# FFN down projection by seven products of block sums in place of eight, alternated with the next block's up products; pieces of 328, 356, 356 tokens

## The chip, the cores and the metric

The kernel runs on one core of one Trainium2 chip. The metric is device time in microseconds (us) of one execution. Before the change three runs took 2256.22, 2258.66 and 2259.83 us; the median is 2258.66. One further execution was recorded by the hardware profiler, and all rows of the profile come from it.

In the profile, PE is TensorE (matmuls), PEld its weight loads, DVE is VectorE, ACT is ScalarE, POOL is GpSimd and SP is SyncE, whose queue issues nearly all DMAs here.

## The reference

One layer of a hybrid encoder: a windowed attention group and a gated linear recurrence (GLA) share an input projection, their outputs go through an output projection, and a feed-forward network (FFN) follows. 2048 prompt tokens and 32 sample tokens are computed, 2080 in all, in fp32, with a model width of 1024 and an FFN width of 4096. Only this end of it is touched by the steps below:

```python
h = x + mixer_output(attn_o, gla_o, rg, g_gla_out, w_out, x.dtype)   # concat(A, B) @ w_out
y = h + ffn(h, g_ffn, w_up, w_down)

def ffn(x, g, w_up, w_down):
    h = rmsnorm(x, g) @ w_up
    return jnp.square(jax.nn.relu(h)) @ w_down
```

## The kernel before

**Arithmetic.** Each fp32 matrix is split into a high part, as TensorE's fp32r type keeps it, and a low part, the remainder. A product is then three matmuls (`mm3`: high x high, low x high, high x low), summed in a PSUM bank. The high part is a copy by ScalarE (line 39 stands for all its activations), the low part a subtraction on GpSimd (weights, lines 1178 and 246) or VectorE (activations, line 1290). All matmuls have line 132.

**Stages.** Attention and the input projection, then GLA, then for each of three *pieces* of tokens the output projection and the FFN. A piece has two groups of N tokens (`gi` 0 and 1), which are the columns of a matmul: N is 320 in piece 0, 360 in pieces 1 and 2. The FFN's 4096 inner channels run in 16 *blocks* `b` of 256.

**Up products.** A block's up projection is a 2 x 2 block product (two halves of the 1024 inputs, two times 128 channels, two token groups), done in seven products (Strassen's scheme in Winograd's form) with sums of weight blocks (S1 to S4, made by GpSimd, line 1180) and sums of token blocks (T1 to T4, made once a piece). Each product is 4 x 3 = 12 matmuls. Its results are named PA11B, PA12B, PS1T, PS2T, PS3T, PA22T and PS4B; VectorE adds them up in PSUM and in `r0` to `r2`, `finished` scales and squares each of the four results in its PSUM bank, and splits it into `uh` and `ul`.

**Down products.** `down` multiplies the four squared results with the block's down weights directly: for each group and each of eight output slices `f`, 2 x 3 matmuls into one bank (`dn`), which VectorE adds to `y` (line 1352). This is a 2 x 2 block product done in eight products of 12 matmuls, 96 matmuls and 16 adds a block.

**Order.** TensorE's program order is the order in which the code is written: five up products of block b, the down products of group 0, the first two up products of block b + 1 (`up_head`), the down products of group 1. The up and down weights of a block are loaded and split again in every piece, a block ahead. The output projection of group 0 of piece 0 (`op0`) is computed before, at the end of GLA.

Of the kernel before, what the change touches and what calls it, by code (L numbers as in the profile page):

```python
# [9 lines left out]
F32 = mybir.dt.float32  # L10
# [9 lines left out]
P = 128  # L20
# [4 lines left out]
EPS = 1e-6  # L25
LEVELS = (64, 32, 16, 8, 4, 2, 1)
# [21 lines left out]
class Builder:  # L48
    def __init__(self, ctx, tc, a, o, nt=NT, ffn=True):
# [9 lines left out]
        self.w = pool("w", 8)  # L59
        self.dram = pool("dram", 1, space=DRAM)  # L60
        self.psm = pool("psm", 3, space=PSUM)
        self.pss = pool("pss", 5, space=PSUM)
# [7 lines left out]
        self.rgd = [dt([self.rows(t), 512], f"rgd{t}") for t in tiles]  # L70

# [16 lines left out]
    def w_tile(self, name):  # L88
        return self.w.tile([P, 2048], F32R, tag="w", name=name)

    def tok_pair(self, name, n):

        return tuple(
            self.tok.tile([P, KB * 320], F32R, tag="tok", name=f"{name}{x}")[:, : KB * n].rearrange(
                "p (k t) -> p k t", k=KB
            )
            for x in "hl"
        )
# [171 lines left out]
    def attention_phase(self):  # L270
# [3 lines left out]
        with ExitStack() as ctx:  # L274
# [337 lines left out]
            for i, t in enumerate(order):  # L612
# [11 lines left out]
                elif i > 1:  # L624
                    z[t] = project_kv(t, *project_q(t))
                if t == nt - 1:
# [30 lines left out]
    def load_gla_consts(self):  # L657
# [16 lines left out]
        self.gla_consts = masks, d0, wal, bal, one, ones  # L674

# [67 lines left out]
    def gla_phase(self):  # L743
        tc, a, V, S, G, Q = self.tc, self.a, self.V, self.S, self.G, self.Q
        nt = self.nt
        with ExitStack() as ctx:
# [272 lines left out]

            for _ in gates(0):  # L1020
                pass
# [14 lines left out]
    def load_wout(self, pi, halves=range(2), engs=(("act", "pool"), ("act", "pool")), after=None):  # L1036
        w_out = self.a["w_out"].rearrange("(k p) n -> p k n", p=P)
        return [self.wide_pairs(w_out, 512 * fh, f"wo{pi}_{fh}", engs, after=after) for fh in halves]
# [52 lines left out]
    def ffn_phase(self, pieces):  # L1091
# [4 lines left out]
        nt = self.nt  # L1096
        NM = max(self.size(g) for p in pieces for g in p)
        H = KB // 2
        with ExitStack() as ctx:

            late = ctx.enter_context(tc.tile_pool(name="late2", bufs=1))
            wk = ctx.enter_context(tc.tile_pool(name="wk2", bufs=1))
            w_up = a["w_up"].rearrange("(k p) n -> p k n", p=P)
            w_dn = a["w_down"].rearrange("(k p) n -> p k n", p=P)
            NF = a["w_up"].shape[1] // 256
# [4 lines left out]
            umem = [[mem(late, NM, f"u{x}{i}") for i in range(4)] for x in "hl"]  # L1110
            cmem = [mem(late, NM, f"cb{i}", F32) for i in range(2)]
            rmem = [mem(late, NM, "r0", F32), mem(late, NM + 160, "r1", F32)]
            ymem = [mem(wk, KB * NM, f"y{gi}", F32) for gi in range(2)]
            tok |= {x: [mem(wk, H * NM, x + y) for y in "hl"] for x in ("T4", "T1", "T2", "B11", "B21")}
            rmem.append(mem(wk, NM, "r2", F32))
# [13 lines left out]

# [11 lines left out]
            def token_sums(name, N, accs):  # L1141
# [4 lines left out]
                q = self.ps_s(f"ss_{name}")[:r]  # L1146
# [7 lines left out]
            def token_scale(name, N, rs, gi):  # L1154

                r, n = rs.shape[0], rs.shape[1] // 2
                rb = self.ps_s(f"rb_{name}_{gi}")[:, :N]
# [5 lines left out]
            def up_weights(b, name, after=None):  # L1163

                raw = []
                for k in range(2):
                    x = self.io_tile("stage")[:, : H * 256].rearrange("p (k c) -> p k c", k=H)
                    self.last_load = Q.dma_start(x, w_up[:, H * k : H * k + H, 256 * b : 256 * b + 256]).ins
                    raw.append(x)
                A = lambda m, k: raw[k - 1][:, :, (m - 1) * P : m * P]  # L1170
                ts = [self.w_tile(f"{name}_{i}").rearrange("p (i x k c) -> p i x k c", i=2, x=2, k=H) for i in range(4)]
                names = ("A11", "A12", "S1", "S2", "S4", "S3", "A22")
                ws = dict(zip(names, ((t[:, i, 0], t[:, i, 1]) for t in ts for i in range(2))))

                def pair(x, src):
                    h, l = ws[x]
                    self.after(S.activation(h, src, AF.Copy), after)
                    G.tensor_tensor(out=l, in0=src, in1=f32(h), op=ALU.subtract)  # L1178

                tt = lambda o, x, y, op: G.tensor_tensor(out=o, in0=x, in1=y, op=op)  # L1180
                pair("A11", A(1, 1))
                pair("A12", A(1, 2))
                pair("A22", A(2, 2))
# [343 lines left out]
```

## Time and profile before

The profiled execution has a span of 2252.4 us. The rows that matter are shown in the prediction. Beside them, the stages of the span, read off the chain of waits by the names of its products:

| stretch, us | what runs |
|---|---|
| 0 to 27 | start-up, waiting for DMA |
| 27 to 360 | input projection and attention |
| 360 to 696 | GLA, and the output projection of group 0 of piece 0 |
| 696 to 778 | output projection of group 1, first FFN block of piece 0 |
| 778 to 1164 | FFN of piece 0 |
| 1164 to 1228 | output projection of piece 1 |
| 1228 to 1707 | FFN of piece 1 |
| 1707 to 1770 | output projection of piece 2 |
| 1770 to 2252 | FFN of piece 2 |

How to read the rows: a row of the timeline or the chain has its start and its length in us, then the engine, the line of the kernel and the result and inputs by the program's names. A group's row ends in count, busy us, mean ns of one and the idle time ahead of it. A window's row has its bounds, then the busy us (and instructions) of PE, PEld, DVE, ACT and POOL, the granted clock of TensorE, DMA's share and GB/s.

### The profile page before, as it was taken

The page shows a single profiled execution, that of the slowest core. Times are in us where ns is not written, and L with a number is a line of the kernel's source. Part 1 is how long each engine was busy: PE and PEld are TensorE (multiplying, and loading weights), DVE is VectorE, ACT ScalarE, POOL GpSimd, SP SyncE. Part 2 cuts the span into 40 slices and gives each one's busy share as a digit, 9 for nine tenths or more (in the row PEclk, how much of TensorE's full clock was granted, in tenths as well). Part 3 has the DMA queues.
Part 4 walks back from the last instruction along what each step waited for, and adds up shares of the span by engine and source line. Part 5 has one row for each costly group of instructions (what it writes and reads, how often), then busy time and mean ns, then how long its engine had stood idle before and what let it go on. Part 6 is the DMA issues. An engine that isn't in the chain of part 4 may idle for free.

```text
span 2252.4 us, 39713 instructions
## 1 busy us (share of the span) xinstructions
PE 2214.7 (98%) x15350; PEld 2088.9 (93%) x15350; DVE 1377.5 (61%) x3554; ACT 967.9 (43%) x2049; POOL 1195.9 (53%) x997
## 2 busy tenths in 40 slices
PE   7999999999989999999999999999999999999999
PEld 6777777888879999999999999999999999999999
DVE  8766665788986655555546555555554655555555
ACT  4555555656665533333335433333325533332331
POOL 4221233333343776677753766666656476666662
PEclk9999999999999999999999999999999999999999
DMA  7332453223143332222262322221227132222221
GB/s 253 137 120 100 172 182 110 100 73 120 62 127 115 95 102 76 76 76 76 68 205 79 101 76 76 75 63 62 65 65 225 57 112 61 63 65 75 76 66 54
DMA packets 156560, 222.98 MB, mean 99 GB/s; under 512 B 38081, under 2 KB 117234, under 8 KB 152530
## 3 DMA queue, kind: packets, MB, share of 16 engines
q1 hardware_dynamic: 156370, 220.43, 30.4%
q8 instruction: 121, 1.98, 0.4%
q14 instruction: 69, 0.57, 0.1%
HBM read 180.82 MB, written 39.57 MB: 98 GB/s over the span
## 4 chain that ended last, share of the span: by engine, by line
PE 91%; DVE 4%; issue 2%; POOL 1%; ACT 1%; DMA 1%; SPq 0%; POOLq 0%; ACTq 0%; DVEq 0%
PE dn L132 31%; PE op L132 8%; PE zq L132 5%; PE zv L132 4%; PE PS2T L132 4%; PE zr L132 4%; PE PS1T L132 4%; PE PA11B L132 4%; PE PA12B L132 4%; PE PS3T L132 4%; PE PA22T L132 4%; PE PS4B L132 4%; PE zkv L132 2%; PE go L132 2%; PE zk L132 2%
## 5 line engine op out<-in xcount | busy, mean ns | idle before, releaser
L1178 POOL TENSOR_TENSOR wu<-stage,wu 128x512 fp32r<-128x512 f32 x336 | 432.4, 1299 | 427.8 <-ACT wu L39 417.4
L1352 DVE TENSOR_TENSOR y<-y,dn 128x360 f32<-128x360 f32 (+1 forms) x768 | 393.2, 515 | 227.0 <-PE dn L132 224.2
L39 ACT ACTIVATE wu<-stage 128x512 fp32r<-128x512 f32 x336 | 206.0, 628 | 494.8 <-PE dn L132 212.0
L1180 POOL TENSOR_TENSOR stage<-stage 128x512 f32<-128x512 f32 x192 | 249.3, 1299 | 7.5
L39 ACT ACTIVATE r<-PA11B 128x360 f32<-128x360 f32 (+1 forms) x48 | 22.0, 458 | 282.3 <-PE PA11B L132 282.3
L887 POOL TENSOR_TENSOR E<-cc 128x256 f32<-128x256 f32 (+1 forms) x117 | 69.5, 630 | 109.6 <-DVE cc L739 51.6
L1290 DVE TENSOR_TENSOR PA12B<-PA12B,r 128x360 f32<-128x360 f32 (+1 forms) x48 | 25.3, 527 | 150.2 <-PE PA12B L132 150.2
L132 PE MATMUL PS2T<-T2h,wu 128*128 128x360 f32 (+1 forms) x384 | 98.8, 321 | 0.7 <-POOL wu L1178 0.7
L132 PE MATMUL PS3T<-T3h,wu 128*128 128x360 f32 (+1 forms) x384 | 99.2, 321 | 0.2 <-ACT T3h L39 0.2
L132 PE MATMUL PA22T<-T4h,wu 128*128 128x360 f32 (+1 forms) x384 | 99.1, 321 | 0.0
L132 PE MATMUL PS4B<-B22h,wu 128*128 128x360 f32 (+1 forms) x384 | 99.1, 321 | 0.0
L132 PE MATMUL PS1T<-T1h,wu 128*128 128x360 f32 (+1 forms) x384 | 98.9, 321 | 0.0
L132 PE MATMUL PA11B<-B11h,wu 128*128 128x360 f32 (+1 forms) x384 | 98.8, 321 | 0.0
L132 PE MATMUL PA12B<-B21h,wu 128*128 128x360 f32 (+1 forms) x384 | 98.7, 321 | 0.0
L963 DVE COPY_PREDICATED AT<-masks,A 64x64 f32<-64x64 int32 (+1 forms) x330 | 82.7, 253 | 19.8 <-ACT AT L39 8.3
L39 ACT ACTIVATE P<-S,negm 128x192 f32<-128x192 f32 (+2 forms) x128 | 51.6, 417 | 45.7 <-DVE negm L553 37.9
L132 PEld LDWEIGHTS PS2T<-T2h,wu 128*128 128x128 f32 x384 | 68.0, 188 | 0.9 <-POOL wu L1178 0.9
L132 PEld LDWEIGHTS PS3T<-T3h,wu 128*128 128x128 f32 x384 | 68.2, 188 | 0.6 <-ACT T3h L39 0.5
L571 POOL TENSOR_TENSOR P<-P,es 128x512 f32<-128x512 f32 x15 | 15.6, 1042 | 98.8 <-ACT sq L39 39.4
L132 PEld LDWEIGHTS PA22T<-T4h,wu 128*128 128x128 f32 x384 | 68.1, 188 | 0.0
L132 PEld LDWEIGHTS PS1T<-T1h,wu 128*128 128x128 f32 x384 | 68.1, 188 | 0.0
L132 PEld LDWEIGHTS PS4B<-B22h,wu 128*128 128x128 f32 x384 | 68.1, 188 | 0.0
(1005 smaller groups left out, 7656.8 us busy)
## 6 DMA issues: line engine op xcount, KB each, us to landing
stage<-in_w_up SPq DMA_DIRECT2D x96, 512.0 KB, 3.8
stage<-in_w_down SPq DMA_DIRECT2D x96, 512.0 KB, 3.9
stage<-in_w_out SPq DMA_DIRECT2D x24, 512.0 KB, 5.7
xT1a<-in_xT_prompt SPq DMA_DIRECT2D x16, 512.0 KB, 4.1
stage<-in_w_in SPq DMA_DIRECT2D x16, 512.0 KB, 4.6
x1a<-in_x_prompt SPq DMA_DIRECT2D x16, 512.0 KB, 5.0
out_yT_prompt<-y SPq DMA_DIRECT2D x32, 180.0 KB, 5.4
m<-mixT SPq DMA_DIRECT2D x11, 512.0 KB, 3.8
```

What stands on the lines that cost most here:

```text
L39: ins = f(*args, **kw)
L132: self._pe(self.T.matmul(out, lhsT, rhs, start=start, stop=stop), ns)
L571: (G if ch == 0 else V).tensor_tensor(out=dst, in0=src, in1=rb, op=ALU.mult)
L887: G.tensor_tensor(out=e4, in0=c4, in1=ref, op=ALU.subtract)
L963: V.copy_predicated(dst, mk.unsqueeze(1).broadcast_to([L // nh, 2, w // m, m]), src[r].rearrange("s p (n m) -> s p n m", m=m),)
L1178: G.tensor_tensor(out=l, in0=src, in1=f32(h), op=ALU.subtract)
L1180: tt = lambda o, x, y, op: G.tensor_tensor(out=o, in0=x, in1=y, op=op)
L1290: tt = lambda out, x, y, op=ALU.add: V.tensor_tensor(out=out, in0=x, in1=y, op=op)
L1352: V.tensor_tensor(out=yg[:, f, :], in0=yg[:, f, :], in1=ps, op=ALU.add)
```

## The change

**Seven down products.** The down projection becomes a 2 x 2 block product too: two halves of the 1024 outputs, two times 128 channels, two groups. A product (`DOWN`: A11, A12, S4, S1, S3, S2, A22) is 12 matmuls into two PSUM tiles of two banks, and VectorE adds each tile, 128 x 2N, to one of seven sums `acc`: four of them are the quarters of `y`, three are new (`P1`, `P6`, `P7`). At a piece's end seven `combine` steps add the sums up, three quarters of each on VectorE and one on GpSimd, and `y` is stored.

**Sums on the token side.** `finished` now squares into SBUF (`F`), and four differences of these results are made by VectorE (T1 to T4), each with both inputs in SBUF. Seven results are split in place of four. The low parts are made by VectorE in piece 0; in pieces 1 and 2 (`easy`) GpSimd makes five of them and VectorE two (T1, T2).

**Sums on the weight side.** `down_sums` makes the block sums of `w_down` on GpSimd ahead of the FFN, during attention and GLA, and keeps them in DRAM (`sd`). Piece 0 makes high and low parts of all down weights, of block 0's up weights, and stores them in DRAM (`kept`), the out weights are stored too (`keep_out`); pieces 1 and 2 load these. The other up weights are split in every piece as before.

**Order.** Down steps of block b - 1 and up steps of block b alternate, one product each, and weights are prepared 7 steps ahead in a ring of 8 tiles. **Pieces** have N = 328, 356 and 356.

```diff
+FIRST, REST = 328, 356
+EARLY = 8
+AHEAD = 7
...
+                if i == 2:
+                    early = [(b, c0, P) for b in range(EARLY) for c0 in range(0, 512, P)]
...
+                    for j in range(2):
+                        self.spawn(self.down_sums(early[j::2], one, 15000), 7500 * j)
...
+    def down_sums(self, units, tile_, gap):
...
+            for k in range(2):
+                self.Q.dma_start(raw[:, k], w[b, :, k, :, c0 : c0 + n])
+            yield gap / 2
+            a11, a21, a12, a22 = raw[:, 0, 0], raw[:, 0, 1], raw[:, 1, 0], raw[:, 1, 1]
+            tt(a22, a21, a22, ALU.add)
+            tt(a21, a11, a21, ALU.subtract)
+            tt(a11, a22, a11, ALU.subtract)
+            tt(a12, a12, a11, ALU.subtract)
+            self.Q.dma_start(self.sd[b][:, :, c0 : c0 + n], raw.rearrange("p k m n -> p (k m) n"))
+            yield gap / 2
...
+            ps1, ps2 = pool("ps1", 4, space=PSUM), pool("ps2", 2, space=PSUM)
+            one = lambda name: ps1.tile([P, 512], F32, tag="one", name=name)
+            two = lambda name: ps2.tile([P, 2, 512], F32, tag="two", name=name)
+            wf, late, wk = pool("wf", 8), pool("late2", 1), pool("wk2", 1)
...
+            DOWN = (("A11", "B11", 1), ("A12", "B21", 2), ("S4", "B22", 3), ("S1", "T1", 5), ("S3", "T3", 7), ("S2", "T2", 6), ("A22", "T4", 4))
...
+            def weights(key, src, keep):
+
+                t = wf.tile([P, 1024], F32R, tag="wf", name=f"wf_{key}")
+                if key in kept:
+                    self.last_load = Q.dma_start(f32(t), kept[key]).ins
+                    return t[:, :512], t[:, 512:]
...
+                S.activation(h, src, AF.Copy)
+                G.tensor_tensor(out=l, in0=src, in1=f32(h), op=ALU.subtract)
+                if keep:
+                    kept[key] = self.dram.tile([P, 1024], F32, tag=f"k{key}", name=f"k{key}")
+                    Q.dma_start(kept[key], f32(t))
...
+                steps = [("U", 0, i) for i in range(7)]
+                for b in range(1, NF):
+                    steps += [(x, b - (x == "D"), i) for i in range(7) for x in "DU"]
+                steps += [("D", NF - 1, i) for i in range(7)]
...
+                def split(x, pool):
+                    h, l = U[x]
+                    src = F["B12" if x == "T3" else "B11" if x == "T1" else "B22" if x == "T2" else "B21" if x == "T4" else x]
+                    S.activation(h, src, AF.Copy)
+                    (G if pool else V).tensor_tensor(out=l, in0=src, in1=f32(h), op=ALU.subtract)
+
+                easy = pi > 0
+
+                def finished(x, ps, add):
+
+                    tt(ps, ps, add)
+                    V.scalar_tensor_tensor(out=ps, in0=ps, scalar=0.0, in1=cb[x in ("B12", "B22")], op0=ALU.max, op1=ALU.mult)
+                    S.activation(F[x], ps, AF.Square)
+                    if x != "B12":
+                        split(x, easy)
+                        return
+                    tt(F["B11"], F["B12"], F["B11"], ALU.subtract)
+                    split("T1", False)
+                    tt(F["B12"], F["B22"], F["B12"], ALU.subtract)
+                    split("T3", easy)
+                    tt(F["B22"], F["B22"], F["B11"], ALU.subtract)
+                    split("T2", False)
+                    tt(F["B21"], F["B21"], F["B22"], ALU.subtract)
+                    split("T4", easy)
...
+                def down(b, i):
+
+                    w, x, q = DOWN[i]
+                    wh, wl = ws["D", b].pop(w)
+                    uh, ul = U[x]
+                    for j in range(0, H, 2):
+                        ps = two(f"dn_{pi}_{b}_{q}_{j}")
+                        for f in range(j, j + 2):
+                            fs = slice(f * P, (f + 1) * P)
+                            self.mm3(ps[:, f - j, :N], wh[:, fs], wl[:, fs], uh, ul, True, True)
+                        ps, at = ps[:, :, :N], acc[q][:, j : j + 2]
+                        if b == 0 and q in (1, 6, 7):
+                            S.activation(at, ps, AF.Copy)
+                        else:
+                            tt(at, at, ps)
...
+                def combine(q, x):
+
+                    for eng, ks in ((V, slice(0, 3)), (G, slice(3, 4))):
+                        eng.tensor_tensor(out=acc[q][:, ks], in0=acc[q][:, ks], in1=acc[x][:, ks], op=ALU.add)
...
-        for n in (320, 360, 360):
+        for n in (FIRST, REST, REST):
```

What stands in a row on VectorE in the steady part of piece 0. Before, from the first up results of block 8 on, the queue holds adds to `y` (`dn_7_1_` is block 7, group 1) and one low part, all with an input in PSUM:

```order
L1290 TENSOR_TENSOR PA12B_0_8_11508<-PA12B_0_8_11508,r_8887 128x320
L1296 SCALAR_TENSOR_TENSOR PA12B_0_8_11508<-PA12B_0_8_11508,cb_8885 128x320
L1352 TENSOR_TENSOR y_8890<-y_8890,dn_7_1_0_11526 128x320
L1352 TENSOR_TENSOR y_8890<-y_8890,dn_7_1_1_11534 128x320
L1290 TENSOR_TENSOR ul_8881<-PA12B_0_8_11508,uh_8877 128x320
L1352 TENSOR_TENSOR y_8890<-y_8890,dn_7_1_2_11542 128x320
```

After the change, from the first down product of block 10 on, the double adds (128x656) have the differences (`fB`) and the low parts (`uT1l` and so on) between them:

```order
L1320 TENSOR_TENSOR P_9317<-P_9317,dn_10_1_0_13075 128x656
L1320 TENSOR_TENSOR fB_9311<-fB_9313,fB_9311 128x328
L1320 TENSOR_TENSOR P_9317<-P_9317,dn_10_1_2_13083 128x656
L1320 TENSOR_TENSOR fB_9313<-fB_9314,fB_9313 128x328
L1481 TENSOR_TENSOR uT1l<-fB_9311,uT1h 128x328
L1320 TENSOR_TENSOR fB_9314<-fB_9314,fB_9311 128x328
L1320 TENSOR_TENSOR y_9323<-y_9323,dn_10_2_0_13113 128x656
L1481 TENSOR_TENSOR uT3l<-fB_9313,uT3h 128x328
L1320 TENSOR_TENSOR fB_9312<-fB_9312,fB_9314 128x328
L1320 TENSOR_TENSOR y_9323<-y_9323,dn_10_2_2_13121 128x656
L1481 TENSOR_TENSOR uT2l<-fB_9314,uT2h 128x328
```

Seven operations with both inputs in SBUF have come between four adds that empty PSUM tiles.

On GpSimd, in the same stage, before: low parts of up weights (`wu`), block sums of `stage`, and two wide low parts of down weights (`wd`) for one block.

```order
L246 TENSOR_TENSOR wd_11l<-stage,wd_11h 128x1024 x2
L1178 TENSOR_TENSOR wu_11_1_12236<-stage,wu_11_1_12236 128x512
L1178 TENSOR_TENSOR wu_11_2_12237<-stage,wu_11_2_12237 128x512
L1178 TENSOR_TENSOR wu_12_0_12514<-stage,wu_12_0_12514 128x512 x2
L1178 TENSOR_TENSOR wu_12_3_12517<-stage,wu_12_3_12517 128x512
```

After, one row for each low part of a block's seven up (`wf_u`) and seven down (`wf_d`) sets, in turn:

```order
L1208 TENSOR_TENSOR wf_d11A_13228<-stage,wf_d11A_13228 128x512
L1208 TENSOR_TENSOR wf_u12A_13253<-stage,wf_u12A_13253 128x512
L1208 TENSOR_TENSOR wf_d11A_13276<-stage,wf_d11A_13276 128x512
L1208 TENSOR_TENSOR wf_u12A_13297<-stage,wf_u12A_13297 128x512
L1208 TENSOR_TENSOR wf_d11S_13319<-stage,wf_d11S_13319 128x512
L1208 TENSOR_TENSOR wf_u12A_13340<-stage,wf_u12A_13340 128x512
L1234 TENSOR_TENSOR stage<-stage 128x4x128 x4
```

The two wide operations on down weights have become seven of 512, put between those on up weights.

On VectorE at the end of the kernel one add stood behind the last down product. Now, from the last product's first add (`dn_15_4_0`) on:

```order
L1320 TENSOR_TENSOR y_9323<-y_9323,dn_15_4_0_25049 128x712
L1575 TENSOR_TENSOR P_9318<-P_9318,P_9317 128x1068
L1320 TENSOR_TENSOR y_9323<-y_9323,dn_15_4_2_25057 128x712
L1575 TENSOR_TENSOR P_9319<-P_9319,P_9318 128x1068
L1575 TENSOR_TENSOR P_9318<-P_9318,y_9324 128x1068
L1575 TENSOR_TENSOR y_9323<-y_9323,P_9319 128x1068
L1575 TENSOR_TENSOR y_9324<-y_9324,P_9319 128x1068
L1575 TENSOR_TENSOR y_9324<-y_9324,P_9318 128x1068
```

Five combinations of 128x1068 stand behind the last add.

More of the change, by code (lines that the diff above doesn't have):

```diff
@@ L1018, in gla_tile @@
                 stage[n] = 4
+            sums = ctx.enter_context(tc.tile_pool(name="sums1b", bufs=2))
+            late = [(b, c0, 256) for b in range(EARLY, self.NB) for c0 in (0, 256)]
+            two = lambda name: sums.tile([P, 1024], F32, tag="sd", name=name)
+            for j in range(2):
+                self.spawn(self.down_sums(late[j::2], two, 32000), 4000 + 16000 * j)
             for _ in gates(0):
@@ L1145, in token_sums @@
                 r = N // n
[L1146 removed]
+                q = two(f"ss_{name}")[:r, 0]
                 ps, q = q[:, : 2 * n], q[:, 2 * n : 4 * n]
@@ new lines, in load, with up_weights @@
+            def load(src):
+                x = self.io_tile("stage")
+                self.last_load = Q.dma_start(x[:, : src.shape[1] * src.shape[2]].rearrange("p (k c) -> p k c", k=src.shape[1]), src).ins
+                return x
+            UP = ("A11", "A12", "S2", "S3", "A22", "S1", "S4")
+            UP0 = ("A11", "A12", "S1", "S2", "A22", "S3", "S4")
+            def up_weights(b, out):
+                order = UP if b else UP0
+                keep = b == 0
+                if f"u{b}A11" in kept:
+                    for x in order:
+                        out[x] = weights(f"u{b}{x}", None, True)
+                        yield
+                    return
+                raw = [load(w_up[:, H * k : H * k + H, 256 * b : 256 * b + 256]).rearrange("p (k c) -> p k c", k=H) for k in range(2)]
@@ L1180, in up_weights @@
-                tt = lambda o, x, y, op: G.tensor_tensor(out=o, in0=x, in1=y, op=op)
+                    out[x] = weights(f"u{b}{x}", lambda: src, keep)
                 pair("A11", A(1, 1))
+                yield
                 pair("A12", A(1, 2))
+                yield
                 pair("A22", A(2, 2))
                 tt(A(2, 2), A(2, 1), A(2, 2), ALU.add)
+                if not b:
+                    pair("S1", A(2, 2))
+                    yield
                 tt(A(2, 1), A(1, 1), A(2, 1), ALU.subtract)
@@ new lines, in banks @@
+                def banks(double, name):
+                    if double:
+                        x = [two(f"{name}{j}") for j in range(2)]
+                        return [x[j // 2][:, j % 2, :N] for j in range(4)]
+                    return None
+                steps = [("U", 0, i) for i in range(7)]
+                for b in range(1, NF):
+                    steps += [(x, b - (x == "D"), i) for i in range(7) for x in "DU"]
+                steps += [("D", NF - 1, i) for i in range(7)]
+                ws = {}
@@ new lines, in combine @@
+                def combine(q, x):
+                    for eng, ks in ((V, slice(0, 3)), (G, slice(3, 4))):
+                        eng.tensor_tensor(out=acc[q][:, ks], in0=acc[q][:, ks], in1=acc[x][:, ks], op=ALU.add)
+                ups = {}
+                for x, b, i in steps:
+                    if x == "U":
+                        if i == 0:
+                            ups[b] = up(b)
+                        next(ups[b])
+                    else:
+                        if (b, i) == (NF - 1, 0) and pi + 1 < len(pieces):
+                            next_mix(pi + 1, 0)
+                            wo_kb[0] = out_weights(0)
+                            next_mix(pi + 1, 1)
+                        down(b, i)
+                        if b == NF - 1 and i == 1:
+                            combine(2, 1)
+                            store(0, range(H))
+                    prepare()
```

348 lines of the change are left out of this document (207 added, 141 removed).

## The prediction

> **What bounds the kernel now.** I read the page's head first, for which engine is full.
>
> ```profile
> span 2252.4 us, 39713 instructions
> PE 2214.7 (98%) x15350; PEld 2088.9 (93%) x15350; DVE 1377.5 (61%) x3554; ACT 967.9 (43%) x2049; POOL 1195.9 (53%) x997
> ```
>
> TensorE is busy 98% of the span; nothing else is near it. Shares are means over unlike stages, so I cut the span into stretches: start-up, and the steady part of the feed-forward network (FFN) in piece 0 (320 columns) and piece 1 (360 columns).
>
> ```profile
> core 0: us, PE busy (x) PEld busy (x) DVE busy (x) ACT busy (x) POOL busy (x), PEclk, DMA share, GB/s
> 0.00:27.00 27.00, 15.26 (x49) 10.38 (x49) 21.54 (x47) 11.99 (x20) 11.71 (x15) 0.99 0.81 265
> 778.00:1122.00 344.00, 344.00 (x2344) 344.00 (x2343) 187.88 (x405) 124.28 (x237) 246.20 (x173) 1.00 0.25 79
> 1260.00:1676.00 416.00, 416.00 (x2527) 416.00 (x2526) 222.52 (x436) 137.16 (x252) 266.53 (x186) 1.00 0.24 75
> ```
>
> In both steady stretches TensorE does not pause, and its granted clock is 1.00. VectorE is at 55% and 53%, GpSimd at 72% and 64%: work taken from TensorE there is taken from the time, as long as the others fit into the shorter block. The chain of waits gives the length of a block, from one group of down products to the same group of the next block.
>
> ```profile
> 778.45 7.04 PE dn L132 x48
> ...
> 804.89 7.04 PE dn L132 x48
> ...
> 1257.41 7.91 PE dn L132 x48
> ...
> 1287.07 7.91 PE dn L132 x48
> ```
>
> A block takes 26.44 us in piece 0 and 29.66 in piece 1. It has 7 x 12 up matmuls and 8 x 12 down matmuls, 180, so one matmul costs 146.9 ns at 320 columns and 164.8 at 360: 0.4475 ns per column. This gives 150.5 ns at 328 and 163.0 at 356.
>
> **Term 1, the eighth product.** A block now has 14 x 12 = 168 matmuls: 25.28 us in piece 0 (was 26.44) and 27.38 in pieces 1 and 2 (was 29.66). Over 16 blocks this is 16 x (1.16 + 2 x 2.28) = **91.5 us less**. The out projections (384 matmuls per piece) keep their sum, since the columns add up to 1040 in both. That is the whole gain; all that follows is what the other engines give back.
>
> **Term 2, VectorE against GpSimd in piece 0.** First VectorE's own load.
>
> ```profile
> L1352 DVE TENSOR_TENSOR y<-y,dn 128x320 f32<-128x320 f32 x208 | 100.7, 487 | 54.7 <-PE dn L132 53.7
> L1352 DVE TENSOR_TENSOR y<-y,dn 128x360 f32<-128x360 f32 x225 | 118.5, 529 | 69.2 <-PE dn L132 68.4
> 737.96 0.48 DVE L1231 TENSOR_TENSOR sums<-sums 128x320 f32<-128x320 f32 x1
> 738.37 0.54 DVE L1236 SCALAR_TENSOR_TENSOR r<-y,packed,r 128x320 f32<-128x320 f32 x1
> 738.83 0.48 DVE L1290 TENSOR_TENSOR PA12B<-PA12B,r 128x320 f32<-128x320 f32 x1
> 739.23 0.47 DVE L1212 TENSOR_TENSOR T2l<-op,T2h 128x320 fp32r<-128x320 f32 x1
> ```
>
> An add from PSUM grows by 42 ns over 40 columns, 1.05 ns per column, so the new add over two banks takes 0.84 us (656 elements) or 0.90 (712). No row shows such an add; it can hardly be dearer than two single ones (0.98), nor cheaper than one (0.49), and I take the slope. A block in piece 0 then has 14 double adds (11.8), 11 operations on up results in PSUM (5.4), and 11 operations with both inputs in SBUF, which the steady state of before has none of: four differences of block results and seven low parts (11 x 0.48 = 5.3). That is 22.5 us by durations; starts follow each other 0.08 sooner than durations say (738.83 to 739.23 is 0.40), so 36 operations could fit in 19.6. I take 21 of 25.28: it fits.
>
> GpSimd, in the same block, makes seven up sets and seven down sets of low weights and four block sums.
>
> ```profile
> L1178 POOL TENSOR_TENSOR wu<-stage,wu 128x512 fp32r<-128x512 f32 x93 | 119.5, 1299 | 95.8 <-ACT wu L39 95.6
> L1180 POOL TENSOR_TENSOR stage<-stage 128x512 f32<-128x512 f32 x54 | 70.0, 1296 | 2.0
> 725.97 1.30 POOL L1178 TENSOR_TENSOR wu<-stage,wu 128x512 fp32r<-128x512 f32 x1
> 727.23 1.30 POOL L1180 TENSOR_TENSOR stage<-stage 128x512 f32<-128x512 f32 x1
> ```
>
> Back to back they start 1.26 us apart, so 18 take 22.8 us of 25.28: it fits too, with 10% to spare. What does not fit is the two together. The timelines of VectorE and GpSimd at the start of piece 0, and in the stretch of the gated recurrence, show why.
>
> ```profile
> 733.85 2.06 POOL L1231 TENSOR_TENSOR sums<-sums,r 128x320 f32<-128x320 f32 x2 [0.29 <-ACT r L39]
> 736.19 0.89 POOL L1231 TENSOR_TENSOR sums<-sums,r 128x320 f32<-128x320 f32 x1 [0.27 <-ACT r L39]
> ...
> 734.05 0.55 DVE L1240 SCALAR_TENSOR_TENSOR op<-y,packed,op 128x320 f32<-128x320 f32 x1
> 734.62 1.64 DVE L1214 SCALAR_TENSOR_TENSOR B22l<-y,packed,B22h 128x320 fp32r<-128x320 f32 x2
> ...
> 737.50 0.54 DVE L1214 SCALAR_TENSOR_TENSOR B22l<-y,packed,B22h 128x320 fp32r<-128x320 f32 x1
> ...
> 600.40 3.74 DVE L871 TENSOR_TENSOR Qc<-kq,ec 128x256 f32<-128x256 f32 x1
> ...
> 598.47 2.36 POOL L887 TENSOR_TENSOR E<-cc 128x256 f32<-128x256 f32 x4
> 600.78 0.62 POOL L879 TENSOR_TENSOR E<-cc 128x256 f32<-128x256 f32 x1
> 601.36 2.51 POOL L787 TENSOR_TENSOR g<-g,ggla 128x512 f32<-128x512 f32 x2
> ```
>
> With GpSimd idle, B22l (two SBUF inputs) takes 0.54; the pair at 734.62, beside two GpSimd operations, takes 1.64, ending 0.35 after GpSimd's pair ends at 735.91, and that pair takes 2.06 in place of 2 x 0.89. Qc, whose neighbours need well under a microsecond, is held for 3.74 and ends 0.27 after GpSimd's last operation ends at 603.87. The operation at 734.05, with one input in PSUM, is not held, nor are the 208 adds above while GpSimd is busy 72% of the time. So an operation with two SBUF inputs waits for the running GpSimd operation and holds the next one up by about 0.28 (2.06 less 2 x 0.89).
>
> The Trainium skill, page "SBUF — State Buffer", section "Who interferes with whom", says it as a rule: a VectorE instruction with two SBUF inputs and a GpSimd instruction that reads SBUF exclude each other for a whole instruction. The trace agrees (3.74 us at 600.40), and there the wait lasted over three GpSimd operations.
>
> The price depends on when the 11 operations arrive. If at random, they wait half a GpSimd operation, 0.63, whenever GpSimd is busy, which is 22.8 + 11 x 0.28 = 25.9 us of the block's length T: T = 21 + 11 x 0.63 x 25.9 / T, so T = 27.5, **2.2 us over TensorE's 25.28**. Bounds: with 19.6 or 22.5 in place of 21, T is 26.4 or 28.7 (1.1 or 3.4); GpSimd alone gives 25.9 (0.6); no exclusion gives 0. Every wait a whole operation gives T = 32 (6.9). I take 2.2 for 15 blocks: **+33**.
>
> **Term 3, the same in pieces 1 and 2.** The down weights come from DRAM here, and GpSimd does five of the low parts: 11 x 1.26 + 5 x about 0.97 (0.89 to 1.03 at 320) = 18.7 of 27.38. VectorE has 14 x 0.90 + 11 x 0.53 + 6 x 0.52 = 21.5 and six waits of 0.63 x 0.7, 24.1: below 27.38, so only a late operation at one place can hold TensorE. Bounds 0 and 0.9 a block (half of the waits straight on TensorE's path); I take 0.3 for 30 blocks: **+9**.
>
> **Term 4, the ends of pieces.** The last block's seven down products have no up products between them, so VectorE's two adds (1.68 to 1.80) stand against a product of 1.81 to 1.96, with eleven or six SBUF operations on top: 3 us a piece without waits, 10, 7 and 4 with whole ones; I take 6, 4 and 3, **+13**. The ring of eight weight tiles is handed to the out projection and refilled: two transitions at 2, **+4**. In piece 0, 8 MB of out weights go to DRAM ahead of the loads of y on SP's queue, beside the chain of differences that already shares VectorE and GpSimd there: **+5** (0 to 10). The start has four more raw loads on SP's queue, where DMA moves 265 GB/s at a share of 0.81, **+2**, and the block sums ahead of the FFN ride on a GpSimd that is half idle, **+2**. The end of the kernel is bare:
>
> ```profile
> 2239.93 8.90 PE dn L132 x54
> 2248.83 0.02 issue
> 2248.85 0.53 DVE y L1352
> ```
>
> Now 0.53 follows the last matmul. After the change a double add (0.9) and five of the six combinations over 1068 elements follow (0.48 + 748 x 1.05 ns = 1.27 each): 7.2, so **+7**. Together 33 (bounds 20 to 47).
>
> **Sum.** 2252.4 - 91.5 + 33 + 9 + 33 = 2235.9 by the profiled execution. The runs' median, 2258.7, lies 6.3 above the span; the same goes on top: **2242 us**.
>
> **Rivals.**
> - *The two engines miss each other.* TensorE's steps pace VectorE, and a wait that ends before TensorE needs the bank costs nothing. Then terms 2 and 3 vanish and term 4 is 27: 2252.4 - 91.5 + 27 + 6.3 = **2194**. For it: both engines fit alone (21 and 22.8 of 25.28). Against: eight of the eleven operations stand close together, and GpSimd is 90% busy.
> - *The exclusion takes the bound (slower).* Operations that stand in a row each meet a freshly started GpSimd operation and wait for all of it, as at 734.62 and 600.40. Midway between half and whole waits, T is about 29.8: 4.5 x 15 = 68, pieces 1 and 2 at 0.9 x 30 = 27, ends 45: 2252.4 - 91.5 + 68 + 27 + 45 + 6.3 = **2307**. It decides from a slip of 3.3 us a block in piece 0 on (15 x 3.3 + 9 + 33 = 91.5). The page's rule named above, taken at its word for every one of the eleven, is this case.
> - *DMA falls behind in piece 0.* A block there loads 2.9 MB and stores 3.7, 6.6 MB in 25.28 us or 260 GB/s. The start row has 265 at a share of 0.81, so some 327 when full: it fits at 80%. If late loads cost 1 us a block, 16 us on top of the forecast, 2258.
>
> **How the numbers follow.** Forecast case 0.37 (its own range, by the bounds of terms 2 and 3, 2215 to 2268), engines missing each other 0.28, exclusion as bound 0.29, DMA 0.06. A measurement of this kernel can tell about 0.2% (4.5 us) from no change. Faster: 0.28 + 0.30 of the forecast case + 0.01; same: 0.04 + 0.02; slower: the rest. The range takes the first rival's time with a little below it, and ends near the second's time, since half of that case lies above: 2190 to 2305.
>
> **What would show it.** Term 1: steady blocks of 168 matmuls, the distance of equal chain rows 27.4 in pieces 1 and 2. Term 2: in piece 0 that distance 27 to 28, VectorE's fB and low-part groups at means near 1.1 us in place of 0.48, and TensorE's idle time ended by VectorE's dn adds; 25.3 with such means would say that the waits are hidden, 29 or more the second rival. Term 3: low-part means above 0.52 with blocks at 27.4 to 27.7. Term 4: 7 us between the last matmul and the last VectorE operation. I would be wrong in kind if idle time of TensorE ended on loads of weights, or if the double add took clearly other than 0.84 to 0.90.

## The result and the profile after

The changed kernel takes 2431.2 us (median of four runs, 2427.7 to 2439.1), the kernel before 2257.5: a ratio of 1.078, 95% interval 1.0755 to 1.0797. It is **slower by 7.8%**; 2242 us was predicted, 2190 to 2305 the range. The profiled execution took 2427.7 us, its span is 2425.7.

The page's head, beside the one shown of before: TensorE has 2211.6 us of work, hardly less than the 2214.7 it had, though a fifteenth of the FFN's matmuls are gone, and its granted clock, at 9 in all slices before, has slices at 8.

```profile
span 2425.7 us, 40665 instructions
...
PE 2211.6 (91%) x14790; PEld 2038.2 (84%) x14790; DVE 1871.4 (77%) x3637; ACT 1009.5 (42%) x2197; POOL 1426.5 (59%) x1360
...
PEclk9999999889989899999999899999999899999998
```

The steady parts of piece 0 and piece 1, in windows as those before: TensorE, never idle there before, is idle 8% and 4% of the time.

```profile
core 0: us, PE busy (x) PEld busy (x) DVE busy (x) ACT busy (x) POOL busy (x), PEclk, DMA share, GB/s
840.00:1260.00 420.00, 387.59 (x2456) 376.37 (x2456) 363.79 (x521) 191.94 (x383) 352.25 (x262) 0.98 0.62 225
1440.00:1800.00 360.00, 345.48 (x2085) 338.20 (x2084) 300.13 (x385) 120.03 (x236) 249.37 (x200) 1.00 0.52 161
```

For the question where the time went, the span is cut by TensorE's own marks in the trace: the first matmul of a stage's products (zk for GLA, op for the out projection, PA11B for the FFN). Each column adds up to its span. "Mended" is the last experiment. e1 to e14 ran once each; ahead of the FFN, where e3 and e4 have the change's code, they came to 698 and 699 us against its 695, so a few us there are chance.

| stage, us | before | after | no sums (e1) | one bank operand (e3) | tiles apart (e4) | mended (e15) |
|---|---|---|---|---|---|---|
| start and attention | 365.7 | 385.5 | 366.1 | 388.9 | 388.2 | 376.6 |
| GLA, to first op | 283.2 | 309.9 | 281.4 | 309.3 | 310.7 | 308.9 |
| out projection, piece 0 | 84.1 | 102.5 | 102.8 | 102.2 | 102.5 | 105.4 |
| FFN, piece 0 | 431.0 | 480.9 | 486.3 | 431.7 | 483.6 | 435.0 |
| out projection, piece 1 | 63.3 | 84.7 | 82.7 | 89.5 | 70.2 | 73.4 |
| FFN, piece 1 | 479.2 | 484.1 | 481.2 | 455.6 | 483.4 | 458.0 |
| out projection, piece 2 | 63.4 | 79.3 | 79.6 | 78.5 | 68.7 | 67.9 |
| FFN, piece 2 | 478.9 | 480.8 | 477.9 | 454.7 | 479.7 | 457.3 |
| behind the last matmul | 3.6 | 18.0 | 18.3 | 18.5 | 18.4 | 16.5 |
| mean block, pieces 0 / 1 | 26.5 / 29.7 | 29.0 / 29.1 | 29.2 / 29.1 | 25.9 / 27.4 | 29.1 / 29.1 | 26.1 / 27.4 |

Every stage is longer than before, those too in which nothing was to be gained. A block of 168 matmuls takes nearly as long as one of 180 in pieces 1 and 2, and longer in piece 0.

What TensorE waits for in these blocks is an add on VectorE. A down product writes two PSUM tiles of two banks; there are only two such tiles, and each is free for the next product when VectorE has added it up. In the window of piece 0 the view of TensorE's waits names these adds (total, number, longest):

```profile
PE dn L135 <- DVE y L1320: 29.3, 27, 2.2
PE dn L135 <- DVE P L1320: 1.9, 6, 0.7
```

In the window of piece 1 it names another operation, uT2h on ACT:

```profile
PE dn L135 <- ACT uT2h L42: 14.5, 12, 1.2
```

The timelines of VectorE and TensorE in one of these blocks show that it is the add here too.

```profile
1507.29 1.62 DVE L1320 TENSOR_TENSOR fB<-fB,fB 128x356 f32<-128x356 f32 x1
1508.84 0.88 DVE L1320 TENSOR_TENSOR P<-P,dn 128x712 f32<-128x712 f32 x1
1509.64 0.82 DVE L1320 TENSOR_TENSOR fB<-fB,fB 128x356 f32<-128x356 f32 x1
1510.38 1.61 DVE L1481 TENSOR_TENSOR uT1l<-fB,uT1h 128x356 fp32r<-128x356 f32 x1
1511.92 1.60 DVE L1320 TENSOR_TENSOR fB<-fB,fB 128x356 f32<-128x356 f32 x1
1513.44 0.88 DVE L1320 TENSOR_TENSOR y<-y,dn 128x712 f32<-128x712 f32 x1
...
1512.93 0.32 PE L135 MATMUL PA12B<-B21h,wf_u5A 128*128 128x356 f32 x1
1514.43 0.40 PE L135 MATMUL dn<-uB22h,wf_d4S 128*128 128x356 f32 x1 [1.18 <-ACT uT2h L42]
```

The product that waits reads uB22h and not uT2h, which ended 0.4 us before. It starts 0.1 us after the add to `y` ends, and so it does in all twelve blocks of the window. That add stands in VectorE's queue behind three differences and one low part, each with both inputs in SBUF, which last 5.65 us in place of some 2.1 (four at 0.53).

### The profile page after: what moved, and what is told of

It is laid out like the page before. It is cut to its first block, busy times and chain, and to the rows that moved or that the text cites. A ratio compares the mean times of both kernels' runs of the same rounds, so it can differ in the third digit from the quotient of the medians.

```text
span 2425.7 us, 40665 instructions
## 1 busy us (share of the span) xinstructions
PE 2211.6 (91%) x14790; PEld 2038.2 (84%) x14790; DVE 1871.4 (77%) x3637; ACT 1009.5 (42%) x2197; POOL 1426.5 (59%) x1360
## 4 chain that ended last, share of the span: by engine, by line
PE 51%; DVE 19%; POOL 11%; DMA 8%; issue 5%; ACT 4%; SPq 1%; DVEq 0%; ACTq 0%; POOLq 0%
PE dn L135 15%; DVE fB L1320 7%; PE op L135 6%; POOL stage L1234 4%; PE PA22T L135 3%; PE PS3T L135 3%; PE PS2T L135 3%; PE PS1T L135 3%; PE zv L135 3%; PE zq L135 3%; PE zr L135 2%; DMA sd<-sd 2%; DVE P L1320 2%; DMA sd<-in_w_down 2%; DVE y L1320 2%
## 5 line engine op out<-in xcount | busy, mean ns | idle before, releaser
L1320 DVE TENSOR_TENSOR y<-y,dn 128x712 f32<-128x712 f32 (+1 forms) x384 | 330.3, 868 | 11.9 <-PE dn L135 5.7
L1320 DVE TENSOR_TENSOR P<-P,dn 128x712 f32<-128x712 f32 (+1 forms) x270 | 235.0, 871 | 27.1 <-PE dn L135 21.9
L1320 DVE TENSOR_TENSOR fB<-fB,fB 128x356 f32<-128x356 f32 (+1 forms) x192 | 204.2, 1063 | 4.9 <-ACT fB L42 2.9
L687 POOL TENSOR_TENSOR sd<-sd 128x128 f32<-128x128 f32 (+1 forms) x192 | 117.5, 628 | 66.4 <-DMA sd<-in_w_down 55.3
L912 POOL TENSOR_TENSOR E<-cc 128x256 f32<-128x256 f32 (+1 forms) x117 | 68.1, 621 | 81.4 <-DVE cc L764 79.6
L1481 DVE TENSOR_TENSOR uT1l<-fB,uT1h 128x356 fp32r<-128x356 f32 (+1 forms) x48 | 69.7, 1452 | 0.0
L42 ACT ACTIVATE E<-E 128x1024 f32<-128x1024 f32 (+2 forms) x68 | 67.2, 1013 | 1.1
L1320 DVE TENSOR_TENSOR PA22T<-PA22T,r 128x356 f32<-128x356 f32 (+1 forms) x48 | 25.3, 527 | 53.0 <-PE PA22T L135 52.9
L135 PE MATMUL op<-T3h,wf_o 128*128 128x356 f32 x128 | 38.4, 373 | 21.9 <-DVE T4l L1327 21.9
L923 DVE TENSOR_TENSOR E<-E,kq 128x256 f32<-128x256 f32 (+1 forms) x117 | 55.0, 522 | 2.0 <-ACT E L42 1.9
L1320 DVE TENSOR_TENSOR r<-PS1T,r 128x356 f32<-128x356 f32 (+1 forms) x48 | 24.8, 516 | 41.1 <-PE PS1T L135 41.1
```

The lines of the kernel that those rows point to most:

```text
L42: ins = f(*args, **kw)
L135: self._pe(self.T.matmul(out, lhsT, rhs, start=start, stop=stop), ns)
L687: tt = lambda o, x, y, op: self.G.tensor_tensor(out=o, in0=x, in1=y, op=op)
L912: G.tensor_tensor(out=e4, in0=c4, in1=ref, op=ALU.subtract)
L923: V.tensor_tensor(out=e4, in0=e4, in1=halves_of(kq, L, m), op=ALU.mult)
L1320: tt = lambda out, x, y, op=ALU.add: V.tensor_tensor(out=out, in0=x, in1=y, op=op)
```

## The experiments

**VectorE against GpSimd (e3).** The squared results stay in their PSUM bank as well, and VectorE's differences and low parts take one operand from there. Two operations a block with both inputs in SBUF are left in piece 0 (of eleven), none in pieces 1 and 2 (of six); GpSimd's work is the same.

```diff
-                    S.activation(F[x], ps, AF.Square)
+                    S.activation(ps, ps, AF.Square)
                     if x != "B12":
-                        split(x, easy)
+                        S.activation(F[x], ps, AF.Copy)
+                        if easy:
+                            split(x, True)
+                        else:
+                            from_bank(x, ps)
                         return
-                    tt(F["B11"], F["B12"], F["B11"], ALU.subtract)
-                    split("T1", False)
-                    tt(F["B12"], F["B22"], F["B12"], ALU.subtract)
+                    tt(F["B12"], F["B22"], ps, ALU.subtract)
+                    tt(ps, ps, F["B11"], ALU.subtract)
+                    from_bank("T1", ps)
                     split("T3", easy)
-                    tt(F["B22"], F["B22"], F["B11"], ALU.subtract)
-                    split("T2", False)
-                    tt(F["B21"], F["B21"], F["B22"], ALU.subtract)
+                    tt(ps, F["B22"], ps, ALU.subtract)
+                    from_bank("T2", ps)
+                    tt(F["B21"], F["B21"], ps, ALU.subtract)
                     split("T4", easy)
+
+                def from_bank(x, ps):
+
+                    h, l = U[x]
+                    S.activation(h, ps, AF.Copy)
+                    tt(l, ps, f32(h), ALU.subtract)
```

> In the FFN the squared results stay in their PSUM bank too, and differences and low parts on VectorE take one operand from there: per block two operations with both inputs in SBUF in piece 0 (eleven before), none in pieces 1 and 2 (six); three more ACT copies. GpSimd's work is unchanged but for nothing. Theory (VectorE waits for GpSimd at operations with two SBUF inputs): blocks of 27.4 to 27.7 us in pieces 1 and 2 (29.1 after the change), 25.4 to 26.5 in piece 0 (28.8), VectorE's differences at means of 0.5 to 0.55 us, time about 2335. Rival (VectorE's queue order and load set the block, whatever its operations read): 28.5 to 29.5 in all pieces. Rival (GpSimd's own chain of weights sets it): pieces 1 and 2 come down, piece 0 stays at 28 or more.

It took 2331.0 us, 100 less than the change's median. The groups of VectorE and GpSimd in the steady part of piece 1, first of the change, then of e3 (the last number ahead of the idle time is the mean in ns):

```profile
L1320 DVE TENSOR_TENSOR fB<-fB,fB 128x356 f32<-128x356 f32 x49 | 56.7, 1157 | 0.0
L1481 DVE TENSOR_TENSOR uT1l<-fB,uT1h 128x356 fp32r<-128x356 f32 x12 | 19.4, 1614 | 0.0
...
L1234 POOL TENSOR_TENSOR stage<-stage 128x512 f32<-128x512 f32 x52 | 69.6, 1339 | 3.1
```

```profile
L1320 DVE TENSOR_TENSOR fB<-fB,PS4B 128x356 f32<-128x356 f32 x26 | 13.4, 517 | 0.0
...
L1320 DVE TENSOR_TENSOR uT1l<-PS4B,uT1h 128x356 fp32r<-128x356 f32 x13 | 6.8, 523 | 0.0
...
L1234 POOL TENSOR_TENSOR stage<-stage 128x512 f32<-128x512 f32 x52 | 67.5, 1298 | 2.0
```

A difference falls from 1157 to 517 ns, the low part of T1 from 1614 to 523, with as many elements and the same GpSimd operations beside them. The window of e3 (columns as above) has TensorE without a gap: 2208 matmuls in 360 us are 163.0 ns each, 27.4 us a block.

```profile
840.00:1200.00 360.00, 355.25 (x2342) 351.30 (x2341) 294.92 (x500) 193.63 (x409) 318.86 (x248) 1.00 0.68 247
1400.00:1760.00 360.00, 360.00 (x2208) 360.00 (x2207) 266.34 (x409) 147.95 (x298) 248.69 (x216) 1.00 0.57 177
```

So the time goes with what a VectorE operation reads; VectorE has as many operations as in the change (3637) and GpSimd too (1360). e3 also makes one difference earlier and no longer overwrites results that GpSimd still reads, but the change's rows show no idle time of VectorE ahead of these operations (0.0): the time was in the operations themselves. DMA, at 247 GB/s in piece 0, does not bound it either.

**The block sums ahead of the FFN (e1, e2, e5, e9, e13).** Waits in GLA of the changed kernel, from 400 to 540 us, from the views of the waits on SP's and GpSimd's queues (total, number, longest), and the end of the longest pause of TensorE there (20 us, to 529), from the chain:

```profile
SPq L698 <- POOL sd L687: 38.1, 13, 7.7
SPq L691 <- DMA sd<-sd: 26.0, 12, 4.5
...
POOL sd L687 <- DMA sd<-in_w_down: 27.1, 12, 11.5
```

```profile
506.20 5.01 DMA sd<-sd
...
511.28 2.96 DMA sd<-in_w_down
...
518.37 0.73 POOL sd L687
...
519.11 0.57 SPq L698
...
521.01 5.72 DMA g<-rgd
...
529.13 3.18 PE go L135 x11
```

A unit's load waits on SP for the store before it, its additions on GpSimd for the load, its store on SP for the additions; g, which GLA needs, stands behind them. e1 leaves the sums out, e2 their additions alone, e13 takes an eighth of the columns of each unit, in the same places:

```diff
-                        self.spawn(self.down_sums(early[j::2], one, 15000), 7500 * j)
-                self.spawn(self.down_sums(late[j::2], two, 32000), 4000 + 16000 * j)
```

> The block sums of w_down are left out: the FFN reads two halves of w_down in their place, in transfers of the same size. Theory (the sums' transfers and additions stand at the head of SP's and GpSimd's queues, and what attention and GLA need waits behind them): the first out matmul, at 695.4 us after the change and 648.9 before, comes back to 647 to 656, and the time falls by 40 to 48 us, to about 2385. Rival (the stages ahead of the FFN lose their time to something else that the change moved there, the smaller weight pools or a lower granted clock): the first out matmul stays above 675.

> The four GpSimd additions of each block-sum unit are left out; its loads and its store stay where they were, so the FFN reads unsummed blocks. Theory (SP's queue: a store waits there for its data and the next load for the store): most of the loss stays, first out matmul at 675 to 695. Rival (GpSimd's additions themselves, their 192 x 0.63 us and their exclusion of VectorE's operations with two SBUF inputs): the first out matmul comes to 650 to 662.

> The block-sum units keep their number, places and waits, but each takes an eighth of its columns (transfers of an eighth of the bytes, additions of an eighth of the width); the FFN reads unsummed halves of w_down in their place. Theory (waits at the head of in-order queues: a transfer's fixed time of some 2 us stays, whatever its bytes): half or more of the loss stays, first out matmul at 670 to 690 (695.4 in the change, 647.5 without sums). Rival (bytes on the DMA engines and GpSimd's time): it comes to 648 to 658.

e5 spreads the units and issues their stores later, with all sums made; e9 issues their transfers from GpSimd's queue:

```diff
-                self.Q.dma_start(raw[:, k], w[b, :, k, :, c0 : c0 + n])
+                self.G.dma_start(raw[:, k], w[b, :, k, :, c0 : c0 + n])
```

> The block sums are made in full, but their units lie further apart (24000 and 70000 in the program's own clock in place of 15000 and 32000), and a unit's store is issued a quarter of that distance behind its additions, its additions a third behind its loads. Theory (waits at the head of SP's and GpSimd's queues): with nearly nothing left to wait for at the head, the first out matmul comes from 695.4 to 650 to 668, time about 2390 to 2405. Rival (the transfers themselves, their bytes on the DMA engines): the bytes are the same, so it stays above 685.

> The block sums as in the change, but their loads and stores are issued from GpSimd's queue in place of SP's. Theory (what attention and GLA wait for are their own transfers, standing in SP's queue behind the sums' loads and stores that wait): SP is free of them, first out matmul at 652 to 672 (695.4 after the change, 647.5 without sums), time 25 to 45 us less. Rival (the sums' bytes on the DMA engines, or GpSimd's queue standing still at their waits): it stays above 685.

| us | before | after | e1 none | e2 no additions | e13 an eighth | e5 spread | e9 GpSimd's queue |
|---|---|---|---|---|---|---|---|
| attention | 365.7 | 385.5 | 366.1 | 392.7 | 390.9 | 380.7 | 376.1 |
| GLA | 283.2 | 309.9 | 281.4 | 295.4 | 285.7 | 331.5 | 310.4 |
| first out matmul | 648.9 | 695.4 | 647.5 | 688.1 | 676.6 | 712.2 | 686.5 |
| whole run | 2257.5 | 2431.2 | 2378.2 | 2425.0 | 2420.6 | 2443.4 | 2418.0 |

Without the units everything comes back: e1 is at 647.5 for the first out matmul, 648.9 before. In attention neither additions nor bytes are the price, since e2 and e13 lose as much there as the change; moving the queue returns half. There, what is left as the cause is the place of the transfers on a queue: the waits at its head, or the time that issuing them takes, which no run tells apart. In GLA the units' length counts: narrow ones cost 2.5 us, those without additions 12. e5 and e9 came out on the side of their rivals, above 685. In e5 the program's own clock bunches the units in GLA however far apart they are asked for, and 25 of the 48 stores came there between 383 and 532 us. e9 shows a second mechanism; the same place of e15, which has this edit, in the timelines of VectorE and GpSimd:

```profile
509.15 14.12 DVE L896 TENSOR_TENSOR Qc<-kq,ec 128x256 f32<-128x256 f32 x1
...
509.16 1.31 POOL L812 TENSOR_TENSOR g<-g,ggla 128x512 f32<-128x512 f32 x1
510.42 2.37 POOL L912 TENSOR_TENSOR E<-cc 128x256 f32<-128x256 f32 x4
512.75 1.27 POOL L812 TENSOR_TENSOR g<-g,ggla 128x512 f32<-128x512 f32 x1
513.99 1.75 POOL L912 TENSOR_TENSOR E<-cc 128x256 f32<-128x256 f32 x3
515.70 0.60 POOL L904 TENSOR_TENSOR E<-cc 128x256 f32<-128x256 f32 x1
516.28 1.42 POOL L687 TENSOR_TENSOR sd<-sd 128x256 f32<-128x256 f32 x2
517.66 4.08 POOL L912 TENSOR_TENSOR E<-cc 128x256 f32<-128x256 f32 x7
521.71 0.60 POOL L904 TENSOR_TENSOR E<-cc 128x256 f32<-128x256 f32 x1
```

One VectorE operation with both inputs in SBUF is held for 14 us, over 20 GpSimd operations that follow each other without a gap (17.8 us in e9, where TensorE then waits 10.0 us for kq, which stands behind it on VectorE). So a part of what was freed on SP is lost here. How the 27 us in GLA divide between the two queues and this exclusion stays open.

**Shared tiles in the out projection (e4, e6, e10).** In piece 1 TensorE pauses twice, for the low part of T4 of the slice just computed; two matmuls start 6.2 and 5.4 us apart there. The waits of TensorE in the change (10.9 us in two, the longer 5.9), and then in e4:

```profile
PE op L135 <- DVE T4l L1327: 10.9, 2, 5.9
```

```profile
PE op L135 <- DVE T4l L1327: 1.9, 1, 1.9
```

```diff
-                        out_mm(bs[f], f + H, 1, range(KB))
-                        second_group(f + H, bs[f])
+                        out_mm(bs[f % 2 * 2 + f // 2], f + H, 1, range(KB))
+                        second_group(f + H, bs[f % 2 * 2 + f // 2])
```

> In the second half of the out projection of pieces 1 and 2, neighbouring output slices go to different two-bank tiles, in place of both banks of one. Theory (the second slice waits for the long chain on the first, since they share a tile, and the clock then falls for some 3 us): the two pauses of 6.2 and 5.4 us and the half-rate stretches behind them go, out projections of pieces 1 and 2 at 68 to 72 us (84.7 and 79.3 after the change), time 22 to 32 us less. Rival (VectorE's chain is what is late, and the wait only moves to the first up products): the sum of out projection and first block falls by less than 8 us a piece.

e4 took 2407.5 us, 24 less; the out projections came to 70.2 and 68.7 us. Two neighbouring slices share a two-bank tile, and the second waited until the first had been worked off. The same thought in piece 0 failed:

```diff
-                            bs = banks(f >= H, f"op1_{f}")
+                            bs = banks(f < H, f"op1_{f}")
```

> In the out projection of group 1 of piece 0 the first four slices go to the two-bank tiles and the last four, which have the long chain behind them, to single banks (the other way round in the change). Theory (shared two-bank tiles, as in the pieces behind): the pauses of 6.8 and 5.1 us go, that stretch falls from 54.7 us to 40 to 45, time about 12 us less. Rival (the chain or the loads of y are late whatever the banks): it stays at 50 or more, or the pauses come back at the first up products.

e6 took 2436.6 us, and that out projection 108.0 (102.5): a pause of 12 us came in place of 6.8. Nor is it the 32 stores ahead of y on SP:

```diff
-                    keep_out(0)
-                    keep_out(1)
...
-                    kbs.append(weights(key, None, True))
+                    kbs.append(weights(f"o{fh}{kb}", lambda: src, False))
```

> The out weights are not stored to DRAM in piece 0; pieces 1 and 2 load them from w_out and split them again (16 ACT copies and 16 GpSimd subtractions a piece). Theory (in piece 0 the loads of y and of out weights stand on SP's queue behind 32 stores): out projection of group 1 of piece 0 falls from 54.7 us to 46 to 50, pieces 1 and 2 stay within 4 us of 84.7 and 79.3 as the splitting has the last block's down products to hide under; time 4 to 10 us less. Rival (four single and four paired banks in place of eight are what is late there): it stays above 52.

e10 took 2444.5 us; piece 0's out projection stayed at 102.3, those behind grew to 93.3 and 86.3. What costs 18 us there is not found. TensorE's two pauses there, 6.8 and 5.1 us from start to start, end on the low part of T4 as in piece 1, and are some 11 of the 18. The rival that e10 names, fewer separate banks than the eight of before, has no run of its own. And e14, whose code is the kernel before's in that stretch, took 90.8 us for it in place of 84.1, so up to 7 us can be chance.

**The granted clock (e14).** In the change, pauses are followed by slow stretches. Windows of piece 1's out projection, a pause and what follows, twice:

```profile
1342.00:1346.00 4.00, 4.00 (x15) 4.00 (x16) 0.00 (x0) 0.00 (x0) 0.00 (x0) 0.54 0.02 4
1346.00:1352.00 6.00, 5.71 (x35) 5.39 (x34) 3.01 (x6) 2.27 (x5) 0.95 (x1) 1.00 0.00 0
1352.00:1357.00 5.00, 0.22 (x1) 0.22 (x2) 3.54 (x7) 2.13 (x5) 0.93 (x1) 0.90 0.00 0
1357.00:1363.00 6.00, 6.00 (x21) 6.00 (x22) 0.00 (x0) 0.47 (x1) 0.00 (x0) 0.52 0.59 187
```

Behind these pauses TensorE is granted about half of its clock for 4 to 6 us, and a matmul takes 295 ns in place of 163. e14 puts such pauses into the kernel before, which has none in its FFN: 16 idle multiplications on one up result, in every second block of piece 1; seven blocks have them (the first is computed by other code).

```diff
+                    for _ in range(hold):
+                        V.tensor_scalar(out=ps, in0=ps, scalar1=1.0, scalar2=None, op0=ALU.mult)
                     S.activation(ps, ps, AF.Square)
```

> The kernel before, with 16 more VectorE operations (a multiplication by 1) on one up result in eight blocks of piece 1, so that TensorE has to wait some microseconds there. Theory (a pause of a few us takes the granted clock down, and TensorE then runs at half rate for some 3.3 us): behind each pause of 2 us or more stands a stretch of matmuls at about 295 ns in place of 165, and the time grows by the pauses and 1.5 us more for each. Rival (the falls of the clock in the changed kernel come from its load, not from its pauses): the clock stays at 1.00 and the time grows by the pauses alone.

```profile
1312.00:1321.00 9.00, 0.33 (x1) 0.29 (x1) 7.67 (x16) 2.09 (x5) 5.60 (x3) 0.74 0.67 204
1321.00:1326.50 5.50, 5.50 (x18) 5.26 (x18) 1.77 (x4) 0.00 (x0) 0.00 (x0) 0.50 0.13 47
1326.50:1340.00 13.50, 13.50 (x83) 13.50 (x83) 6.58 (x13) 2.55 (x5) 2.55 (x2) 1.00 0.01 2
```

The clock is 0.50 behind the pause, then 1.00 again. Piece 1's FFN grew from 479.2 to 561.8 us: seven pauses of 9.05 us (from start to start, less one matmul) are 63 of the 83, and 2.8 a pause are the clock's and the restart's. So here the falls follow from the pauses. A short pause by itself did not bring one: the twelve of 1.2 us, one a block, in the change's window of piece 1 left the clock at 1.00. In the change, the FFN and the out projections have 21 stretches of four and more matmuls that start 240 to 340 ns apart, 72 us; at 163 in place of 295 ns they would take 40, so some 32 us of the loss are this. The Trainium skill, page "TensorE: Matmul & The Clock Gate", Part 1, has a half-rate state after an idle window of about 3.4 us and a release after one of work. The 0.50 agrees; the idle window does not, since in the change pauses of 1.4, 1.2 and 0.9 us close together, at 1281 us, were enough.

**All together (e7, e8, e15).** e7 joined e3 to e6 with VectorE alone at the combinations, e8 the same without sums (a bound; the FFN reads unsummed halves of w_down), e12 had the edits of e9 and e10 in place of e5 and e6, and e15 is e12 without e10.

> All that left the outputs whole so far together: one operand from the bank, tiles apart in pieces 1 and 2, sums spread, single banks in piece 0, and the combinations at a piece's end by VectorE alone. If the mechanisms are separate their gains add: 97 + 24 + 30 + 12 + about 2, from 2431 to 2260 to 2275. If they share one cause (the granted clock falling in any pause) the sum is smaller and the time stays above 2290.

> As the run before it, but the block sums are left out (the FFN reads unsummed halves of w_down in their place). It prices what is left without them: 2431 - 97 - 50 - 24 - 12 - 2, 2240 to 2255, at or a little below the kernel before (2258). If blocks stand at 27.4 and 25.9 and it is still at 2250, what is left lies between the steady stretches: starts and ends of pieces, out projections, the tail.

> One operand from the bank, tiles apart in pieces 1 and 2, combinations on VectorE alone, out weights split again and the sums on GpSimd's queue, all outputs whole. If the gains add: 2431 - 97 - 24 - 2 - 7 - 35 = 2266, range 2255 to 2290; at the kernel before (2257) or under it only if the pauses that go with several causes at once vanish too. Blocks at 27.4 in pieces 1 and 2 and 26 in piece 0, out projections at 68 to 72.

> One operand from the bank, tiles apart in pieces 1 and 2, combinations on VectorE alone, sums on GpSimd's queue; out weights stored as in the change; all outputs whole. Without the splitting of out weights, which cost 13 us by itself, 2301 falls to 2285 to 2298. Rival (that cost was hidden once the exclusion is gone): 2299 to 2305. Either way above the kernel before.

e7 took 2329.5, e8 2272.7 and e12 2301.0 us. e15 took 2299.5 (ratio to before 1.019, interval 1.016 to 1.021). All four came out above the time expected of them; e15 lies in its rival's range. The gains of e3 and e4 add up, those ahead of the FFN do not. Even e8, without sums, is above the kernel before (2256 beside it), so no version here beats it.

## Why the prediction was wrong, step by step

The span moved by +173.3 us; the sum foresaw -16.5. By the table:

- **Term 1** (-91.5) was right. e3 gives 27.4 us a block at a granted clock of 1.00, the 27.38 worked out.
- **Term 2** (+33) had the mechanism, VectorE's waits for GpSimd, and missed the size: (29.0 - 25.28) x 15 = 56. The step that failed is the formula in which VectorE is the full engine and each wait lengthens the block: VectorE was busy 363.8 of 420 us, 87%, and the eleven operations waited about 4.8 us a block (a difference took 1.00 us in place of 0.49, a low part 0.74 to 1.22), less than the 6.5 put in. They stand ahead of the adds that free PSUM tiles, so TensorE waits although VectorE has idle time elsewhere. TensorE's idle time in that window is 32.4 us, 2.2 a block, and that this equals the term is luck. On top, its 2456 matmuls took 18.0 us more than at 150.5 ns, 1.2 a block, at a granted clock of 0.98; the term had nothing for that.
- **Term 3** (+9) failed in its bound, "0.9 a block (half of the waits straight on TensorE's path)", from which 0.3 was taken. The place was as said, one late operation, but it held TensorE in every block: (29.1 - 27.38) x 30 = 51. Each of six operations was to wait 0.44 us, 2.6 in all; four that stand in a row ahead of the add to `y` waited 3.5 in the block shown, all on that add's path. Half of 2.6 would have been 1.3 besides, not 0.9. A sum of work below the block's length says nothing about how long one add stands in the queue.
- **Term 4, start and sums** (+4 for raw loads and additions) failed at "ride on a GpSimd that is half idle": 46.5 us in attention and GLA. Their place on two in-order queues, ahead of other stages' transfers, was not walked through; without them the 46.5 are gone (e1).
- **Term 4, between the pieces** (+4) failed likewise: 37.3 in two out projections, of which e4 returned 25.1. That two slices share one tile was not in the working at all. Piece 0's out projection (+5) has 18.4 more; its cause is open.
- **Term 4, ends of pieces** (+13): what is left of the FFN stages' change, once terms 1 to 3 are taken out as measured, is 41; what makes it up was not taken apart. **The tail** (+7) is 14.4: the last combinations take 1.9 us each in place of 1.27, beside GpSimd's share of them, and the stores come behind.

```profile
2409.45 1.19 DVE P L1575
...
2410.67 1.88 DVE P L1575
2412.55 1.92 DVE y L1575
```

With the 41 as the remainder these add up: -91.5 + 56 + 51 + 46.5 + 37.3 + 18.4 + 41 + 14.4 = 173. The clock's fall is in them: the forecast priced every pause at its own length.

Of the rivals, the exclusion as the bound was nearest in kind, at 2307: operations in a row that each wait for most of a GpSimd operation are what the block shown has. "The engines miss each other" is refuted by the means of 1.00 and 1.16 us and by e3, and DMA did not fall behind. (By its own bounds of terms 2 and 3 the forecast case reached to 2278, not 2268.) The range was too narrow because its bounds were those of terms 2 and 3, while 125 of the 190 us missed lie in term 4.

## What to carry to other kernels

Before work is moved to VectorE beside a busy GpSimd, count the operations with both inputs in SBUF, and look which of them stand in a row ahead of one that frees a PSUM tile; where one operand could stay in PSUM, the wait was gone (e3). Work that is hidden by an idle engine still stands in line: walk through what is queued behind its waits, on the DMA-issuing engine first. And a kernel at 98% TensorE has a granted clock to lose: matmuls at half rate came behind pauses of several us, and behind shorter ones close together.

## What the runs showed of the hardware that was not expected

The wait of a VectorE operation with two SBUF inputs is not bounded by one GpSimd operation: 14.1 and 17.8 us were measured over a gapless row of them. A pause of TensorE cost 2.8 us beyond its own length (e14), and the stretch behind it ran at a granted clock of 0.50.
